# Half 0's scan groups 1 and 2 as one output product of eight k tiles, with the merge's first part stepped as its sums are finished

## The chip, the cores and the metric

The kernel runs on one core of one Trainium2 chip. The metric is the device time of one execution in microseconds (us); less is better.

## What is computed

One inference step of a small hybrid model: a SwiGLU block, then two branches (a pooling mixer and a Mamba-2 scan, "SSD") that sigmoid gates join, then a second SwiGLU block. All is float32. There are 1024 prompt tokens and 64 sample tokens (8 sequences of 8), `D_MODEL` is 1024. The change lies in the part behind the scan:

```python
yg = (y.reshape(Bsz, T, D_INNER) * jax.nn.silu(z))
yg = yg.reshape(Bsz, T, N_SSD_GROUPS, D_INNER // N_SSD_GROUPS)      # 4 groups of 512
yg = yg * lax.rsqrt(jnp.mean(yg * yg, axis=-1, keepdims=True) + EPS)
y = yg.reshape(Bsz, T, D_INNER) * ssd_norm
branch_ssd = y @ ssd_w_out                                          # 2048 x 1024
gates = jax.nn.sigmoid(gate_logits).reshape(Bsz, T, 2, D_MODEL)
merged = gates[:, :, 0] * branch_pool + gates[:, :, 1] * branch_ssd
return merged @ w_o, ...
```

## The kernel before

**Tiling.** Activations lie transposed, channels on the 128 partitions, tokens along the free dimension. The tokens are two halves: half 0 has 512 prompt tokens, half 1 the other 512 and the 64 sample tokens (576). A block of 128 channels is a k tile or, of an output, an m block. Each product of float32 numbers is made of three matmuls: every operand is split into a high and a low part (`split`, L370 on ScalarE for the high one, L374 on VectorE for the low one), and high x high, low x high and high x low are summed in PSUM (`products`). In half 0 an m block's sum takes one PSUM bank; four banks, of the kind `pd`, go round.

**The scan and its output product.** The scan goes through eight pieces in a fixed order, half 0's groups 0 to 3 and then half 1's. A group of the reference is four k tiles of `branch_ssd`'s product. The scan is a chain: a generator that is stepped in between the matmuls of the products (`tick`), each `yield x` saying after how many us of emitted matmuls the next step is due. So while TensorE makes half 0's output products, half 1's group 0 is scanned. In the profile the scan's names are `pxT`, `pcb`, `pst`, `pyo`, `pyd` (PSUM), `xdt`, `xd`, `ab`, `ea`, `cbm`, `hst` (VectorE and GpSimd). Behind the scan of each group comes `gating`: the gate (L1677), the sum of squares on VectorE (`ssq`, L395) and TensorE (`pss`), its root on GpSimd (`rsm`, L378), spread by TensorE (`prb`, L180), and the four splits (`yhl`, L374). The operands `yhl` lie in buffers of the kind `pair`, of which there are 8, one for a k tile's two parts: two groups at a time. The line `while h * NG + g - 2 >= freed[0]` holds the splits of a group back until the group two before it has been used by its output product; `freed` counts the groups used.

**SETS.** Of each half, `SETS` says which groups make an output product together. Half 0 has four sets of one group. The first three are made by `ssd_out`: for each of the eight m blocks a sum over four k tiles, which is put into `acc[m]` by ScalarE for group 0 (L1760) and added to `acc[m]` by VectorE for the others (L1762). `dense` loads the weights in two transfers for each m block and group. The last set is made by `merge`.

**The merge.** With t = 2 x sigmoid - 1 of the gate, kept in DRAM as `gd`, and the pooling branch's gated part as `accd`, it makes (t + 1) x (acc + pso) + ac. Its first part, `head`, is a chain of eight steps, one for each m block: load `t1` and `ac` (L1774, L1775; 256 KB each), then 2 us later on VectorE acc = (t1 + 1) x acc (L1777), and on GpSimd acc = acc + ac (L1778). It starts when the merge starts. The second part, for each m block: the sum `pso` over group 3's four k tiles, on VectorE t1 = (t1 + 1) x pso (L1791) and t1 = t1 + acc (L1792), and the split into `mh` and `ml` by 0.5, the operands of the next product (`pwo`, with `w_o`), whose sums use the same four `pd` banks.

**Order.** The order of each engine's instructions is set when the program is built: by the order in which the code and the chains emit them, and by a scheduler with priorities (`tc.high_priority`: evictions, HP_EV, go ahead). SyncE issues nearly all transfers in the order of its own queue.

## Time and profile before

| | |
|---|---|
| median of 3 runs | 2871.04 us (2869.55 to 2874.98) |
| the profiled execution's own time | 2877.41 us |
| its span in the trace | 2875.6 us |
| mean granted TensorE clock | 0.989 |
| output product of groups 1 and 2, half 0 | about 1714 to 1787 us of the span, for the part that follows group 1's first three blocks |
| merge of half 0 | 1787 to about 1850 us |

Engines are PE (TensorE's matmuls), PEld (its weight loads), DVE (VectorE), ACT (ScalarE), POOL (GpSimd) and SP (SyncE). PEclk is the TensorE clock that was granted, as a share of full speed. A group's row gives line, engine, operation, output and inputs, shapes and count, then the busy time in us, the mean in ns, and the idle time of the engine ahead of it with what ended most of that. A row of the timeline gives the start and the duration in us, and in brackets the idle time ahead of it and what ended it. A row of the waits gives who waited for whom: us in total, times, longest.

### The profile page before, as it was taken

What the parts mean: (1) busy time and instruction counts of PE and PEld (TensorE: products, weight loads), DVE (VectorE), ACT (ScalarE), POOL (GpSimd) and SP (SyncE); (2) the same over time, 40 slices, a digit from 0 to 9 for tenths busy, and PEclk for the clock granted to TensorE, in tenths of its full rate; (3) what the DMA queues carried; (4) which work ended last, traced back from release to release, by engine and by line L of the source; (5) the groups of instructions that cost most, each with busy time, mean ns of one, the idle gap of its engine ahead of it and who ended that gap; (6) DMA issues with size and microseconds to landing.
All of it is one profiled execution on the core that took longest, in us unless ns stands there. A gap on an engine that the chain in (4) does not pass through costs nothing.

```text
span 2875.6 us, 54690 instructions
## 1 busy us (share of the span) xinstructions
PE 2775.5 (97%) x19834; PEld 2606.6 (91%) x19834; DVE 1879.0 (65%) x2912; ACT 1364.5 (47%) x3024; POOL 1378.5 (48%) x1406
## 2 busy tenths in 40 slices
PE   7999999999999999999989999899999999999998
PEld 5999999899889999999988887678999999998997
DVE  6665565777884586867765767776665554457675
ACT  5444444643454565554554446556233434445433
POOL 6566566543442355554622332332235766664522
PEclk9999999999999999999999999999999999999999
DMA  4565554787745455544377788887775332337865
GB/s 132 180 209 193 175 161 151 248 295 250 238 130 161 154 167 168 180 155 137 100 234 231 213 251 268 261 272 216 235 242 176 107 99 94 99 114 257 286 202 183
DMA packets 533488, 548.02 MB, mean 191 GB/s; under 512 B 42836, under 2 KB 373704, under 8 KB 533208
## 3 DMA queue, kind: packets, MB, share of 16 engines
q1 hardware_dynamic: 533200, 544.51, 59.5%
q8 instruction: 156, 2.56, 0.4%
q14 instruction: 116, 0.95, 0.1%
q10 hardware_dynamic: 16, 0.00, 0.0%
HBM read 391.82 MB, written 152.78 MB: 189 GB/s over the span
## 4 chain that ended last, share of the span: by engine, by line
PE 75%; DMA 7%; DVE 6%; issue 4%; POOL 4%; ACT 2%; SPq 1%; POOLq 0%; ACTq 0%; DVEq 0%
PE pw L176 43%; PE po L176 10%; PE pso L176 5%; PE pg L176 3%; PE pbp L176 3%; PE pwo L176 3%; PE pu L176 2%; DMA hr<-xq 1%; PE pgm L176 1%; DMA hp<-xq 1%; PE pyd L176 1%; PE pst L176 1%; DVE hr L781 1%; DVE wl L459 1%; POOL s L676 1%
## 5 line engine op out<-in xcount | busy, mean ns | idle before, releaser
L176 PE MATMUL pw<-X,wh 128*128 128x288 f32 (+2 forms) x2832 | 627.5, 310 | 5.0 <-ACT t L604 2.7
L176 PEld LDWEIGHTS pw<-X,wh 128*128 128x128 f32 x2832 | 462.1, 189 | 27.3 <-ACT t L604 3.2
L176 PE MATMUL pw<-X,wl 128*128 128x288 f32 (+1 forms) x1644 | 473.6, 288 | 0.8 <-DVE wl L459 0.8
L459 DVE TENSOR_TENSOR wl<-s,wh 128x512 fp32r<-128x512 f32 x288 | 245.2, 853 | 247.1 <-ACT wh L458 232.4
L176 PE MATMUL pw<-hl,wh 128*128 128x256 f32 (+1 forms) x1536 | 391.7, 328 | 3.6 <-ACT t L580 2.3
L452 POOL TENSOR_TENSOR s<-wraw,wraw 128x512 f32<-128x512 f32 x144 | 198.9, 1381 | 332.8 <-DVE wl L459 210.3
L176 PE MATMUL pw<-hi,wh 128*128 128x288 f32 x1120 | 331.7, 296 | 2.6 <-DVE t L616 1.9
L176 PE MATMUL pw<-hi,wl 128*128 128x288 f32 x1120 | 329.8, 294 | 0.0
L176 PE MATMUL pw<-lo,wh 128*128 128x288 f32 x1120 | 329.6, 294 | 0.0
L176 PEld LDWEIGHTS pw<-X,wl 128*128 128x128 f32 x1644 | 311.7, 190 | 1.0 <-DVE wl L459 1.0
L176 PE MATMUL pw<-hl,wl 128*128 128x256 f32 x1072 | 300.6, 280 | 0.9 <-DVE wl L459 0.9
L176 PEld LDWEIGHTS pw<-hl,wh 128*128 128x128 f32 x1536 | 258.8, 189 | 24.9 <-ACT t L580 2.9
L759 POOL TENSOR_TENSOR ws<-wraw,wraw 128x512 f32<-128x512 f32 x120 | 179.8, 1507 | 200.9 <-DMA wraw<-in_ffn_w_out_dram 88.5
L459 DVE TENSOR_TENSOR wl<-wraw,wh 128x512 fp32r<-128x512 f32 x216 | 185.3, 858 | 124.2 <-ACT wh L458 118.9
L458 ACT ACTIVATE wh<-s 128x512 fp32r<-128x512 f32 x288 | 181.2, 630 | 136.2 <-PE pw L176 110.0
L176 PEld LDWEIGHTS pw<-hi,wh 128*128 128x128 f32 x1120 | 210.5, 188 | 9.5 <-DVE t L616 2.5
L176 PEld LDWEIGHTS pw<-lo,wh 128*128 128x128 f32 x1120 | 210.6, 188 | 0.0
L176 PEld LDWEIGHTS pw<-hi,wl 128*128 128x128 f32 x1120 | 210.1, 188 | 0.0
L458 ACT ACTIVATE wh<-wraw 128x512 fp32r<-128x512 f32 x216 | 135.8, 629 | 151.4 <-PE pw L176 130.7
L176 PEld LDWEIGHTS pw<-hl,wl 128*128 128x128 f32 x1072 | 202.9, 189 | 1.9 <-DVE wl L459 1.9
L176 PE MATMUL po<-hh,wh 128*128 128x272 f32 x848 | 179.9, 294 | 10.1 <-ACT wh L767 8.7
L176 PE MATMUL po<-hr,wh 128*128 128x272 f32 x848 | 178.1, 291 | 3.8 <-DVE hr L781 3.8
(403 smaller groups left out, 6773.3 us busy)
## 6 DMA issues: line engine op xcount, KB each, us to landing
wraw<-in_ffn_w_out_dram SPq DMA_DIRECT2D x240, 256.0 KB
wraw<-in_ffn_w_in_dram SPq DMA_DIRECT2D x188, 256.0 KB
wraw<-in_w_in_dram SPq DMA_DIRECT2D x144, 256.0 KB
wh<-part SPq DMA_DIRECT2D x116, 256.0 KB
wl<-part SPq DMA_DIRECT2D x116, 256.0 KB
hr<-xq SPq DMA_DIRECT2D x106, 272.0 KB
xq<-s SPq DMA_DIRECT2D x66, 272.0 KB
xq<-g SPq DMA_DIRECT2D x62, 272.0 KB
```

The lines of the kernel that those rows point to most:

```text
L176: T.matmul(out, lhsT, rhs, start=start, stop=stop, skip_group_check=free)
L452: G.tensor_tensor(t, a, b, op=op)
L458: S.activation(wh, a, AF.Copy)
L459: V.tensor_tensor(wl, a, wh.bitcast(F32), op=ALU.subtract)
L676: G.tensor_tensor(out[:, a], x0[:, a], y[:, b0], op=op)
L759: G.tensor_tensor(s, raws[0], raws[1], op=ALU.subtract if p in MINUS2 else ALU.add)
L781: V.tensor_tensor(t[:, :n].bitcast(F32R), t[:, :n], a[:, :n].bitcast(F32), op=ALU.subtract)
```

## The change

`SETS` of half 0 becomes (0), (1, 2), (3). `ssd_out` is written anew: for a set of several groups the first `N_LEAD` m blocks (three in half 0, one in half 1) are done group by group, with their banks kept open, so that the second group's operands are needed only behind three blocks of the first; the other blocks run over all k tiles at once. Each m block of groups 1 and 2 is then one sum of eight k tiles and one eviction into `acc[m]` where there were two: eight VectorE adds fewer in half 0. The number of matmuls and of weight loads stays. `freed` goes from 1 to 3 at once at the joint product's end.

`head` becomes `merge_head`. In half 0 it starts ahead of the joint product and not with the merge, and a step waits until its m block's sum has been evicted (`left`): the sixteen loads, the eight L1777 and the eight L1778 stand between the joint product's matmuls. In half 1 it starts where it did, ahead of the merge. From line 57 on, lines are one higher in the new kernel; L1777 and L1778 become L1763 and L1764, L1791 and L1792 become L1807 and L1808, the add of an eviction, L1762, becomes L1790.

```diff
-SETS = (((0,), (1,), (2,), (3,)), ((0, 1), (2,), (3,)))
+SETS = (((0,), (1, 2), (3,)), ((0, 1), (2,), (3,)))
+N_LEAD = (3, 1)
...
-    def ssd_out(h, gs, acc):
-
-        yn = ynorm(h, gs)
-        for m in range(KD):
-            pb = dense(ssd_w_out[0], gs[0] * 4, 4 * len(gs), m * P, [yn], name="pso")[0]
...
-        def head():
+    def merge_head(h, acc, left):
+
+        N, t1, count = NTOK[h], [None] * KD, [0]
+
+        def run():
             for m in range(KD):
                 t1[m], ac = act((P, N), name="t1"), act((P, N), name="ac")
                 dma(t1[m], gd[h][KD + m])
                 dma(ac, accd[h][m])
                 yield MP
+                while left[0] <= m:
+                    yield 1.0
                 V.scalar_tensor_tensor(acc[m], t1[m], 1.0, acc[m], op0=ALU.add, op1=ALU.mult)
                 G.tensor_tensor(acc[m], acc[m], ac, op=ALU.add)
-                merged[0] += 1
-
-        ch = start(head(), MP)
+                count[0] += 1
+
+        return start(run(), MP), t1, count
+
+    def ssd_out(h, gs, acc, left):
+
+        lead = N_LEAD[h] if len(gs) > 1 else 1
+        for ms in (tuple(range(lead)),) + tuple((m,) for m in range(lead, KD)):
+            pbs = [banks([(h,)], "pd", "pso")[0] for _ in ms]
+            for i, g in enumerate(gs):
+                _, yh, yl = scanned(h, g)
+                before_ = [None] * (4 * i)
+                for m, pb in zip(ms, pbs):
+                    wh, wl = load_w(ssd_w_out[0], g * 4, 4, m * P)
+                    for kk in range(4):
+                        products([pb], wh, wl, kk, slice(0, P), [(h, before_ + yh, before_ + yl)], 4 * i + kk, 4 * len(gs))
+                        tick()
...
+                left[0] += 1
+        freed[0] += len(gs)
+
+    def merge(h, gs, acc, first):
+
+        N = NTOK[h]
+        ch, t1, merged = first
...
         for gs in SETS[h][:-1]:
-            ssd_out(h, gs, acc)
-        mhl = merge(h, SETS[h][-1], acc)
+            left = [0]
+            if h == 0 and gs == SETS[h][-2]:
+                first = merge_head(h, acc, left)
+            ssd_out(h, gs, acc, left)
+        if h == 1:
+            first = merge_head(h, acc, left)
+        mhl = merge(h, SETS[h][-1], acc, first)
```

How the instructions move, at three places of VectorE's order. The first is the end of the product ahead of the merge. Before, from the last eviction (of `pso` into `acc_3881`, the eighth m block) on; all operands of the merge have been split by then:

```order
L1762 TENSOR_TENSOR acc_3875_21747<-acc_3875_21747,pso_22689 128x512
L1541 TENSOR_TENSOR ab_22629<-ab_22629,cbm_22663 128x512
L1541 TENSOR_TENSOR ab_22631<-ab_22631,cbm_22663 128x512
L1762 TENSOR_TENSOR acc_3881_21783<-acc_3881_21783,pso_22715 128x512
L395 TENSOR_TENSOR ssq_22733<-ssq_22733,sq_22735 128x576
L1638 TENSOR_TENSOR hst_22752<-hst_22752,pst_22750 128x512
L1520 TENSOR_TENSOR xdt_22767<-pxT_22755,dts_20160 128x512
L1513 TENSOR_TENSOR cbm_22763<-pcb_22760,tri 128x128
L1530 TENSOR_TENSOR xd_22769<-pxT_22755,dts_20160 128x512
L1541 TENSOR_TENSOR ab_22707<-ab_22707,cbm_22763 128x512
L1541 TENSOR_TENSOR ab_22709<-ab_22709,cbm_22763 128x512
```

After, the four splits of group 3 (`yhl` of 128x512) stand here:

```order
L375 SCALAR_TENSOR_TENSOR yhl_22753<-xs_3684_20737,cols,yhl_22753 128x512
L1542 TENSOR_TENSOR ab_22641<-ab_22641,cbm_22673 128x512
L375 SCALAR_TENSOR_TENSOR yhl_22757<-xs_3684_20737,cols,yhl_22757 128x512
L1542 TENSOR_TENSOR ab_22643<-ab_22643,cbm_22673 128x512
L1790 TENSOR_TENSOR acc_3881_21783<-acc_3881_21783,pso_22699 128x512
L396 TENSOR_TENSOR ssq_22747<-ssq_22747,sq_22749 128x576
L375 SCALAR_TENSOR_TENSOR yhl_22761<-xs_3684_20737,cols,yhl_22761 128x512
L375 SCALAR_TENSOR_TENSOR yhl_22765<-xs_3684_20737,cols,yhl_22765 128x512
L1521 TENSOR_TENSOR xdt_22799<-pxT_22787,dts_20160 128x512
L1514 TENSOR_TENSOR cbm_22795<-pcb_22792,tri 128x128
L1531 TENSOR_TENSOR xd_22801<-pxT_22787,dts_20160 128x512
L1807 SCALAR_TENSOR_TENSOR t_3899_21847<-t_3899_21847,pso_22769 128x512
```

Two of the splits come ahead of the last eviction and two behind it, and the first L1807 of the merge has moved ahead of the scan's `hst`.

The second place is the merge's start, from the last sum of squares of half 1's group 0 (`ssq`) to its mean (`rsm`), which the steps behind `prb` need. Before:

```order
L395 TENSOR_TENSOR ssq_22733<-ssq_22733,sq_22787 128x576
L1617 TENSOR_TENSOR ea_22633<-pyo_22823,ea_22633 128x512
L1777 SCALAR_TENSOR_TENSOR acc_3810_21468<-t_4100_22790,acc_3810_21468 128x512
L1618 TENSOR_TENSOR ea_22633<-ea_22633,pyd_22828 128x512
L1791 SCALAR_TENSOR_TENSOR t_4100_22790<-t_4100_22790,pso_22739 128x512
L1777 SCALAR_TENSOR_TENSOR acc_3822_21520<-t_4102_22802,acc_3822_21520 128x512
L1792 TENSOR_TENSOR t_4100_22790<-t_4100_22790,acc_3810_21468 128x512
L1513 TENSOR_TENSOR cbm_22883<-pcb_22880,tri 128x128
L1791 SCALAR_TENSOR_TENSOR t_4102_22802<-t_4102_22802,pso_22812 128x512
L374 SCALAR_TENSOR_TENSOR ml_22807<-t_4100_22790,mh_22806 128x512
L407 TENSOR_SCALAR rsm_22859<-pss_22853 128x4
L409 TENSOR_SCALAR rsm_22859<-pss_22853 64x1
```

After:

```order
L396 TENSOR_TENSOR ssq_22747<-ssq_22747,sq_22816 128x576
L1808 TENSOR_TENSOR t_3899_21847<-t_3899_21847,acc_3810_21468 128x512
L396 TENSOR_TENSOR ssq_22747<-ssq_22747,sq_22819 128x576
L1807 SCALAR_TENSOR_TENSOR t_3963_22145<-t_3963_22145,pso_22834 128x512
L375 SCALAR_TENSOR_TENSOR ml_22829<-t_3899_21847,mh_22828 128x512
L1618 TENSOR_TENSOR ea_22645<-pyo_22845,ea_22645 128x512
L408 TENSOR_SCALAR rsm_22875<-pss_22869 128x4
L1619 TENSOR_TENSOR ea_22645<-ea_22645,pyd_22850 128x512
L410 TENSOR_SCALAR rsm_22875<-pss_22869 64x1
```

Nine instructions stood between the last `ssq` and the first `rsm`, and three do now; an L1808 has come in ahead of that `ssq`.

The third place is the middle of the merge, from `hst` on, where the merge's `ml` and the evictions of `pso` stand among the scan's and the gating's instructions. Before:

```order
L1638 TENSOR_TENSOR hst_23010<-hst_23010,pst_23008 128x512
L1777 SCALAR_TENSOR_TENSOR acc_3863_21694<-t_4147_22983,acc_3863_21694 128x512
L374 SCALAR_TENSOR_TENSOR yhl_23058<-xs_3787_21312,cols,yhl_23058 128x576
L1792 TENSOR_TENSOR t_4126_22906<-t_4126_22906,acc_3846_21624 128x512
L1777 SCALAR_TENSOR_TENSOR acc_3875_21747<-t_4163_23044,acc_3875_21747 128x512
L1617 TENSOR_TENSOR ea_22844<-pyo_23085,ea_22844 128x512
L374 SCALAR_TENSOR_TENSOR ml_23066<-t_4126_22906,mh_23065 128x512
L1513 TENSOR_TENSOR cbm_23137<-pcb_23135,tri_s 64x64
L1618 TENSOR_TENSOR ea_22844<-ea_22844,pyd_23090 128x512
L1791 SCALAR_TENSOR_TENSOR t_4135_22941<-t_4135_22941,pso_23071 128x512
L1791 SCALAR_TENSOR_TENSOR t_4147_22983<-t_4147_22983,pso_23197 128x512
L1791 SCALAR_TENSOR_TENSOR t_4163_23044<-t_4163_23044,pso_23220 128x512
```

After:

```order
L375 SCALAR_TENSOR_TENSOR yhl_23050<-xs_3787_21312,cols,yhl_23050 128x576
L1808 TENSOR_TENSOR t_3977_22210<-t_3977_22210,acc_3846_21624 128x512
L1618 TENSOR_TENSOR ea_22866<-pyo_23071,ea_22866 128x512
L1807 SCALAR_TENSOR_TENSOR t_4009_22326<-t_4009_22326,pso_23063 128x512
L1514 TENSOR_TENSOR cbm_23121<-pcb_23119,tri_s 64x64
L375 SCALAR_TENSOR_TENSOR ml_23058<-t_3977_22210,mh_23057 128x512
L1619 TENSOR_TENSOR ea_22866<-ea_22866,pyd_23076 128x512
L1807 SCALAR_TENSOR_TENSOR t_4018_22383<-t_4018_22383,pso_23181 128x512
L1807 SCALAR_TENSOR_TENSOR t_4053_22559<-t_4053_22559,pso_23204 128x512
```

The two L1777 here (of `acc_3863` and `acc_3875`, the sixth and seventh m block) are gone; in the new order they stand ahead of the merge, as do the other six but the last, which stands just behind its first product.

More of the change, by code (lines that the diff above doesn't have):

```diff
@@ L1748, in ynorm @@
         return h, sum((y[1] for y in ys), []), sum((y[2] for y in ys), [])
-    def ssd_out(h, gs, acc):
-        yn = ynorm(h, gs)
-        for m in range(KD):
-            pb = dense(ssd_w_out[0], gs[0] * 4, 4 * len(gs), m * P, [yn], name="pso")[0]
-            if gs[0] == 0:
-                acc[m] = act((P, NTOK[h]), name="acc2")
-            with tc.high_priority(HP_EV):
-                for pt, (a, b) in zip(pb, PIECES[h]):
-                    if gs[0] == 0:
-                        S.copy(acc[m][:, a:b], pt[:, : b - a])
-                    else:
-                        V.tensor_tensor(acc[m][:, a:b], acc[m][:, a:b], pt[:, : b - a], op=ALU.add)
-        freed[0] += len(gs)
-    def merge(h, gs, acc):
-        N = NTOK[h]
-        t1 = [None] * KD
-        merged = [0]
-        def head():
+    def merge_head(h, acc, left):
+        N, t1, count = NTOK[h], [None] * KD, [0]
+        def run():
             for m in range(KD):
@@ L1776, in head @@
                 yield MP
+                while left[0] <= m:
+                    yield 1.0
                 V.scalar_tensor_tensor(acc[m], t1[m], 1.0, acc[m], op0=ALU.add, op1=ALU.mult)
                 G.tensor_tensor(acc[m], acc[m], ac, op=ALU.add)
-                merged[0] += 1
-        ch = start(head(), MP)
+                count[0] += 1
[12 more added lines that the diff above has]
+                        tick()
+            for m, pb in zip(ms, pbs):
+                if gs[0] == 0:
+                    acc[m] = act((P, NTOK[h]), name="acc2")
+                with tc.high_priority(HP_EV):
+                    for pt, (a, b) in zip(pb, PIECES[h]):
+                        if gs[0] == 0:
+                            S.copy(acc[m][:, a:b], pt[:, : b - a])
+                        else:
+                            V.tensor_tensor(acc[m][:, a:b], acc[m][:, a:b], pt[:, : b - a], op=ALU.add)
+                left[0] += 1
[3 more added lines that the diff above has]
+        ch, t1, merged = first
         yn = ynorm(h, gs)
```

## The prediction

> **What bounds the kernel now.** I read the page first, for what is busy over the whole span.
>
> ```profile
> span 2875.6 us, 54690 instructions
> PE 2775.5 (97%) x19834; PEld 2606.6 (91%) x19834; DVE 1879.0 (65%) x2912; ACT 1364.5 (47%) x3024; POOL 1378.5 (48%) x1406
> ```
>
> TensorE is busy in 97% of the span, and the change leaves its matmuls as they are. Time can come only from stretches in which TensorE waits, or runs at a lower granted clock. So the next view is the sums by windows for the three stretches that the change touches: the second and third groups' product of half 0 (1714 to 1787), the merge of half 0 (1787 to about 1850), and what follows it.
>
> ```profile
> core 0: us, PE busy (x) PEld busy (x) DVE busy (x) ACT busy (x) POOL busy (x), PEclk, DMA share, GB/s
> 1714.00:1787.00 73.00, 71.42 (x481) 56.80 (x480) 57.09 (x90) 44.09 (x122) 27.12 (x24) 1.00 0.87 262
> 1787.00:1850.00 63.00, 55.08 (x297) 41.90 (x296) 55.69 (x82) 29.73 (x77) 29.25 (x21) 0.92 0.84 278
> 1850.00:1910.00 60.00, 55.46 (x378) 41.88 (x378) 41.53 (x65) 37.40 (x101) 20.74 (x16) 1.00 0.85 263
> ```
>
> In the first stretch TensorE is idle for 73.00 - 71.42 = 1.6 us only. In the merge it is idle for 63.00 - 55.08 = 7.9 us, its clock is granted at 0.92 (worth up to 63 x 0.08 = 5.0 us), and VectorE has 55.69 us of work in 63. So at most 7.9 + 5.0 = 12.9 us can be had in the merge. The waits of TensorE in these two stretches, the merge's first, say who ends the idle time:
>
> ```profile
> PE prb L180 <- POOL rsm L378: 2.2, 1, 2.2
> PE pst L176 <- DVE xd L1530: 2.1, 1, 2.1
> PE pwo L176 <- DVE t L1791: 2.1, 1, 2.1
> PE pcb L176 <- DVE ea L1617: 0.7, 1, 0.7
> PE pwo L176 <- DVE ml L374: 0.6, 1, 0.6
> ```
>
> ```profile
> PE prb L180 <- POOL rsm L378: 0.8, 1, 0.8
> PE ph0T L180 <- DMA h<-in_state_ssm_dram: 0.8, 1, 0.8
> ```
>
> Four of the merge's five waits are for VectorE, 5.5 us together; the fifth is for a small GpSimd step. In the earlier stretch neither wait is for an eviction.
>
> **The evictions.** Eight adds of a 128x512 sum into `acc` go. The groups by line in the earlier stretch:
>
> ```profile
> L1762 DVE TENSOR_TENSOR acc<-acc,pso 128x512 f32<-128x512 f32 x15 | 10.2, 680 | 2.5 <-PE pso L176 2.5
> L374 DVE SCALAR_TENSOR_TENSOR yhl<-xs,cols,yhl 128x512 fp32r<-128x512 f32 x4 | 3.0, 746 | 0.4 <-ACT yhl L370 0.4
> ```
>
> They free 8 x 0.68 = 5.4 us of VectorE. VectorE is idle there for 73.00 - 57.09 = 15.9 us and no wait of TensorE is for it, so I count them at nothing. If that cover were gone they would be worth the 5.4.
>
> **The merge's first part.** In the merge it is these rows, of VectorE and of GpSimd:
>
> ```profile
> L1777 DVE SCALAR_TENSOR_TENSOR acc<-t,acc 128x512 f32<-128x512 f32 x8 | 6.5, 808 | 0.0
> L1778 POOL TENSOR_TENSOR acc<-acc,ac 128x512 f32<-128x512 f32 x8 | 13.6, 1707 | 17.3 <-DVE acc L1777 17.3
> ```
>
> 6.5 us of VectorE and 13.6 of GpSimd leave the merge for the joint product, with 16 loads of 256 KB. Not all of the 6.5 pays: an instruction counts only where VectorE runs without a gap and TensorE waits at its end. That is the stretch from 1816.13 to 1835.94, here by its first row, some inside, and its last, the third of three together:
>
> ```profile
> 1816.13 0.29 DVE L1513 TENSOR_TENSOR cbm<-pcb,tri 128x128 f32<-128x128 f32 x1 [3.12 <-PE pcb L180]
> 1820.11 1.85 DVE L1686 TENSOR_TENSOR xs<-xs,r 128x576 f32<-128x576 f32 x1
> 1825.33 0.75 DVE L1686 TENSOR_TENSOR xs<-xs,r 128x576 f32<-128x576 f32 x1
> 1827.93 0.68 DVE L1530 TENSOR_TENSOR xd<-pxT,dts 128x512 f32<-128x512 f32 x1
> 1832.26 1.17 DVE L374 SCALAR_TENSOR_TENSOR ml<-t,mh 128x512 fp32r<-128x512 f32 x1
> 1834.08 1.86 DVE L1791 SCALAR_TENSOR_TENSOR t<-t,pso 128x512 f32<-128x512 f32 x3
> ```
>
> Three of TensorE's waits end on its rows:
>
> ```profile
> 1828.75 2.05 PE L176 MATMUL pst<-xd,btok 128*128 128x512 f32 x2 [2.09 <-DVE xd L1530]
> 1832.39 0.33 PE L176 MATMUL pcb<-bc,bc 128*64 128x64 f32 x2 [0.74 <-DVE ea L1617]
> 1834.80 0.50 PE L176 MATMUL pwo<-mh,wh 128*128 128x512 f32 x1 [2.08 <-DVE t L1791]
> ```
>
> By the order, 27 instructions stand behind that `cbm` up to the third L1791; after the change 23 do. Three L1777 are gone, and one add to `ea` stands ahead of the `cbm`, where VectorE sits idle for 3.12 us. At the 0.6 us from one to the next (three in 1.86), that is 4 x 0.6 = 2.4 us. More goes with the GpSimd adds. Two of them run here:
>
> ```profile
> 1819.66 1.68 POOL L1778 TENSOR_TENSOR acc<-acc,ac 128x512 f32<-128x512 f32 x1 [1.30 <-DVE acc L1777]
> 1829.88 4.66 POOL L1778 TENSOR_TENSOR acc<-acc,ac 128x512 f32<-128x512 f32 x2 [7.02 <-DVE acc L1777]
> ```
>
> The L1686 that begins beside the first takes 1.85 us against 0.75 without one (1.1 more), and `ml` beside the second 1.17 against the 0.68 of its neighbours (0.5 more). The Trainium skill, page "SBUF — State Buffer", section "SBUF: two separate sides", says that a VectorE instruction with two inputs in SBUF and a GpSimd instruction that reads SBUF hold one pair of ports in turn, the loser fully blocked. The trace agrees by its sign, with 1.1 us; by that rule the price isn't removed but goes with the adds into the earlier stretch, which is the slower rival below.
>
> So VectorE is done here 2.4 + 1.6 = 4.0 us earlier. Of TensorE's 2.09 + 0.74 + 2.08 = 4.9 us, 4.0 go; about 0.9 at the first `pwo` stays. Behind it, one L1777 less in VectorE's queue takes 0.6 us, the `ml` wait.
>
> **From the merge's start to `prb`.** Here the change adds. The last of group 3's four splits before, and the merge's first product with its third k tile:
>
> ```profile
> 1762.52 0.75 DVE L374 SCALAR_TENSOR_TENSOR yhl<-xs,cols,yhl 128x512 fp32r<-128x512 f32 x1 [0.40 <-ACT yhl L370]
> 1787.10 0.61 PE L176 MATMUL pso<-yhl,wh 128*128 128x512 f32 x2
> 1790.00 0.70 PE L176 MATMUL pso<-yhl,wh 128*128 128x512 f32 x2
> ```
>
> The splits were done 24 us ahead of that product; now they stand right ahead of the merge's first product, since its buffers come free only as the joint product's last sum reads group 1 for the last time. Four splits of 0.75 are 3.0 us, two of them behind the last eviction, which waits for that sum. TensorE needs the third of them only 2.9 us into the merge (two k tiles and the scan's steps lie between), when the last eviction, an `ssq` add and that split (0.7 + 0.75 + 0.75) are just done, so it waits 0 to 1 us for them. But the `ssq` sums are queued behind them on VectorE, and `pss` waits for those:
>
> ```profile
> 1793.31 1.61 DVE L395 TENSOR_TENSOR ssq<-ssq,sq 128x576 f32<-128x576 f32 x2
> 1795.07 1.23 PE L176 MATMUL pss<-ones,ssq 128*128 128x1 f32 x10
> 1799.13 1.74 POOL L1778 TENSOR_TENSOR acc<-acc,ac 128x512 f32<-128x512 f32 x1
> 1802.29 1.62 POOL L378 TENSOR_TENSOR rsm<-rsm,mhalf 128x5 f32<-128x5 f32 x1
> 1803.96 0.32 PE L180 MATMUL prb<-ident,rsm 128*128 128x128 f32 x1 [2.15 <-POOL rsm L378]
> ```
>
> By the order VectorE has two splits, an L1791, an L1777 and an L1792 more between the last eviction and the last `ssq`: 2 x 0.75 + 3 x 0.6 = 3.3 us. `ssq` ended at 1794.92, just ahead of `pss`, so `pss` waits up to 3 us where it waited for nothing. What is lost there is mostly given back at `prb`: behind the last `ssq`, nine instructions stood ahead of `rsm` on VectorE and three do now (two L1777, an L1791, an L1792 and two steps of the scan are elsewhere), and the add of 1.74 us isn't ahead of it on GpSimd. So `pss` waits 2 to 3, `prb` 0.5 to 1 instead of 2.15: net **+1 us**, between -1.5 (no new wait) and +3 (nothing given back).
>
> **The clock.** Two windows of 5 us in the merge, and one in the stretch before:
>
> ```profile
> 1805.00:1810.00 5.00, 5.00 (x16) 3.93 (x16) 3.93 (x7) 2.36 (x7) 2.39 (x3) 0.68 0.96 327
> 1835.00:1840.00 5.00, 5.00 (x20) 4.00 (x20) 4.68 (x7) 1.34 (x5) 4.10 (x4) 0.66 0.99 279
> 1770.00:1775.00 5.00, 4.21 (x31) 2.91 (x32) 1.80 (x3) 5.00 (x16) 0.00 (x0) 1.00 1.07 337
> ```
>
> Behind the 2.15 us wait at 1803.96 and behind the three that end at 1834.80 TensorE is busy throughout at 0.68 and 0.66, so each costs 5 x 0.33 = 1.6 us. Behind idle time of 0.8 us, at 1770, the clock stays at 1.00. If the second group of waits shrinks from 4.9 to 0.9 its dip goes: **-1.6 us**. The first I leave, as `pss` and `prb` still wait some 3 us. The Trainium skill, page "TensorE: Matmul & The Clock Gate", section "What's actually happening", has the clock fall after at least one idle window of some 3.4 us in a free-running frame; the longest single wait here is 2.15 us, so by it neither dip should be there, this term would be 0, and the sum 1.6 us less. The rows show both, and I go by them.
>
> **The joint product.** It takes the eight steps on VectorE and GpSimd and 16 loads into a stretch whose transfers have a share of 0.87 and a clock at 1.00. VectorE's sum there moves little (-5.4 for evictions, +6.5 for eight steps). What can be late are the state load at 0.8 us (its issue is queued behind more loads on SP) and GpSimd's steps on the carried state. No row before shows it; the nearest are the two 0.8 us waits. From 0 to three such more, 2.4; I take **+0.5**. Group 2's use costs nothing: it is read first after three blocks of group 1, at the place in TensorE's order where group 1's fourth block stood, so later than before.
>
> **Sum.** -4.0 - 0.6 + 1.0 - 1.6 + 0.5 = -4.7, say -5, and the order behind the merge is the same, so that it carries through to the end. The profiled execution took 2877.41 us, 6.4 more than the median of the runs, 2871.04; against the median -5 gives **2866 us**. About 0.2% (5.7 us) is what a measurement here can tell from no change, so the forecast lies just inside.
>
> **Rivals.**
> - *The clock and `prb` come back in full.* If TensorE's wait at `pss` doesn't appear (VectorE has idle time that takes the splits), `prb` falls to the 0.8 us of the earlier stretch and both dips go: -4.9 - 0.6 - 1.4 - 3.2 - 1 for the later stretch = -11, 2860 us. For it: the earlier stretch holds the same scan steps at 1.00. Against: 3.3 us more are queued ahead of `ssq`. Chance 0.15.
> - *The relief is eaten by the next wait.* TensorE gets to `pwo` 3 us earlier and waits there for `ml` or for the state chain of half 1; the dip stays. Then -4.0 - 0.6 + 2 + 1.6 = -1, 2870 us. For it: three waits in a row that all end on one engine. Chance 0.12.
> - *Slower: GpSimd's adds hold up half 1's scan.* The eight adds, 13.6 us, stand in the joint product ahead of GpSimd's steps on the carried state and the gate, which TensorE needs within each scan unit; each add also blocks one VectorE step by 1.1 us. If 11 us of these 13.6 + 8.8 lie on the path, that outweighs the -4.7 and gives +6, 2877 us; it decides from 0.6 us of new wait per add. Against it: in the merge GpSimd's adds held TensorE once in eight times, at `prb`. Chance 0.13.
> - That the change doesn't do what it says is excluded by the order, which has eight evictions fewer and the steps moved.
>
> **Numbers.** The likeliest case has 0.60; its own range is +1 to -9 by the bounds above (-4.6 + 3 + 2.4, and -4.6 - 1.5 - 3.2), somewhat less than half of it beyond 5.7. Faster: 0.28 + 0.15 = 0.43. Same: 0.32 + 0.12 = 0.44. Slower: 0.13. The range goes from some 14 us below the median, past the first rival, to 3 above, which leaves out most of the slower one: 2857 to 2874.
>
> **What would show it.** Right: no `pst<-xd` wait near 2 us and no dip behind the merge's second half; `prb` under 1.2; a new `pss<-ssq` wait of 2 to 3; 1714 to 1787 no more than 1 us longer. Wrong: `pwo` waiting 3 us or more, or TensorE's idle time in the joint product over 4 us.

## The result, and the profile after

The changed kernel takes 2866.77 us (median of 20 runs, 2860.67 to 2876.58) against 2871.27 (20 runs, 2865.16 to 2876.78): a ratio of 0.9982, 95% interval 0.9975 to 0.9989, or 4.5 us less by the medians and 5.2 by the ratio. Two more comparisons with further runs gave 0.9990 (0.9981 to 0.9999) and 0.9993 (0.9984 to 1.0002), that is 2.9 and 2.0 us less, the last with 1 inside its interval. The prediction was 2866, 5 us less. Its number came out, much of its working did not.

The profiled execution took 2863.49 us. The page's first lines, after:

```profile
span 2861.7 us, 54691 instructions
PE 2766.0 (97%) x19834; PEld 2595.6 (91%) x19834; DVE 1867.4 (65%) x2904; ACT 1362.0 (48%) x3024; POOL 1367.7 (48%) x1406
```

The eight adds are gone (2912 to 2904 instructions on VectorE). The sums by windows, in the same three stretches as before the change:

```profile
1714.00:1787.00 73.00, 69.25 (x468) 54.25 (x466) 57.63 (x84) 40.17 (x114) 34.19 (x29) 1.00 0.91 283
1787.00:1850.00 63.00, 56.23 (x313) 42.03 (x313) 54.47 (x85) 34.33 (x89) 16.96 (x15) 0.97 0.81 251
1850.00:1910.00 60.00, 56.78 (x397) 43.02 (x395) 42.92 (x68) 34.66 (x94) 22.01 (x17) 0.97 0.86 267
```

In the joint product TensorE is idle for 3.75 us (1.6 before), in the merge for 6.8 (7.9 before), and the merge's clock is 0.97 where it was 0.92. GpSimd's work in the merge fell from 29.25 to 16.96 us, VectorE's hardly (55.69 to 54.47): the stretch now gets further into the work behind it. The waits of TensorE after, in the joint product and in the merge:

```profile
PE pb L181 <- DVE hst L1639: 0.8, 1, 0.8
PE px L181 <- DVE xdt L1521: 0.7, 1, 0.7
PE pst L177 <- DVE xd L1531: 0.7, 1, 0.7
PE prb L181 <- POOL rsm L379: 0.6, 1, 0.6
PE px L181 <- DVE ea L1619: 0.6, 1, 0.6
PE pb L181 <- DVE cbm L1514: 0.4, 1, 0.4
```

```profile
PE pss L181 <- POOL rsm L379: 2.3, 1, 2.3
PE pso L177 <- DVE yhl L375: 1.7, 2, 1.2
PE pso L177 <- DMA wl<-part: 1.0, 1, 1.0
PE pst L177 <- DVE xd L1531: 0.7, 1, 0.7
...
```

The waits of 2.1 us at `pst` and `pwo` are a third of what they were or gone. In their place stand five new ones for VectorE's scan steps in the joint product (3.2 us together), two at the merge's first product for the late splits, one for weights, and the one for `rsm` is as long as before.

**Where the time went.** A trace's stretches can be compared to a few tenths of a microsecond, where the clock falls at the same places, if they are cut at the scan's steps, which every variant has, and not at times. I take the time since the `pst` at 1710.55 us (of before; 1707.34 after), add or subtract 0.227 us for each 512-column product matmul that the variant has done fewer or more by then (three of them take 0.68 us from one k tile's row to the next), and subtract the same of the first trace of before. Positive is late. Three traces of each kernel, by the time of before at which the step stands:

```
step, at us of before      before 1   2      3     after 1   2      3
state step ph0T    1764.2    0.00   0.28  -0.15     3.79   3.84   3.82
last group's pcb   1780.6    0.00   0.21   0.46     2.31   2.36   2.34
pst in the merge   1788.5    0.00   0.21   0.45     4.04   4.08   4.05
prb                1804.0    0.00   0.21   0.45     8.21   8.18   8.43
pst behind prb     1813.6    0.00   0.15  -1.17     6.15   6.11   6.35
ph0T, merge's end  1844.2    0.00   0.30  -0.88    -0.75  -0.77  -0.55
pcb                1871.7    0.00   0.03  -1.11    -1.05  -0.66  -0.97
pcb                1938.2    0.00  -0.67  -1.13    -0.85  -1.58  -2.36
pcb                1966.3    0.00  -0.88  -1.22    -3.98  -3.78  -5.19
```

The change loses 2.3 us in the joint product, 1.7 at the merge's first product, 4.1 more up to `prb`, and wins 9.0 from there to the merge's end. Some 2 us of the 4.1 and of the 9.0 are a dip of the clock (a stretch at half speed) that has changed its place. Before, it lies just behind `prb` (1805 to 1810 at 0.68, and in the third trace not at all); after, it lies just ahead of it, in all three traces:

```profile
1800.00:1805.00 5.00, 5.00 (x20) 3.53 (x20) 2.86 (x7) 0.00 (x0) 0.00 (x0) 0.66 1.10 306
```

At the `pst` behind `prb` both have had theirs: by that cut the change loses 2.1 us from the merge's first product on and wins 6.9 from there. At the merge's end half a microsecond is left (0.75, 1.07 and -0.33 by pairs). A further 3 us are won behind the merge, up to 1966, and 2.0 in the second SwiGLU block: from the last `pwo` to that block's first `po` the three traces before take 477.7, 477.8 and 477.7 us, the three after 475.4, 475.7 and 476.0.

### The profile page after: what moved, and what is told of

It reads as the page before. It is cut to its first block, busy times and chain, and to the rows that moved or that the text cites. A ratio compares the mean times of both kernels' runs of the same rounds, so it can differ in the third digit from the quotient of the medians.

```text
span 2861.7 us, 54691 instructions
## 1 busy us (share of the span) xinstructions
PE 2766.0 (97%) x19834; PEld 2595.6 (91%) x19834; DVE 1867.4 (65%) x2904; ACT 1362.0 (48%) x3024; POOL 1367.7 (48%) x1406
## 4 chain that ended last, share of the span: by engine, by line
PE 74%; DMA 9%; DVE 6%; issue 4%; POOL 3%; ACT 3%; SPq 1%; POOLq 0%; ACTq 0%; DVEq 0%
PE pw L177 45%; PE po L177 8%; PE pso L177 4%; PE pg L177 3%; PE pbp L177 3%; PE pwo L177 3%; PE pu L177 2%; DMA hr<-xq 2%; DMA hp<-xq 1%; DMA ea<-eacd 1%; DMA wraw<-in_ffn_w_out_dram 1%; PE pgm L177 1%; DMA ab<-acsd 1%; DVE hr L782 1%; PE pyd L177 1%
## 5 line engine op out<-in xcount | busy, mean ns | idle before, releaser
L760 POOL TENSOR_TENSOR ws<-wraw,wraw 128x512 f32<-128x512 f32 x120 | 172.0, 1440 | 204.4 <-DVE wl L769 74.7
L460 DVE TENSOR_TENSOR wl<-wraw,wh 128x512 fp32r<-128x512 f32 x216 | 178.3, 825 | 125.3 <-ACT wh L459 120.5
L177 PE MATMUL pso<-yhl,wh 128*128 128x288 f32 (+1 forms) x768 | 179.2, 338 | 2.1 <-DVE yhl L375 1.7
```

The source lines that it names most:

```text
L177: T.matmul(out, lhsT, rhs, start=start, stop=stop, skip_group_check=free)
L460: V.tensor_tensor(wl, a, wh.bitcast(F32), op=ALU.subtract)
L760: G.tensor_tensor(s, raws[0], raws[1], op=ALU.subtract if p in MINUS2 else ALU.add)
```

## The experiments

One table for all, read like the one above:

```
                            1764   1780   1788   1804   1844   1966   ratio of the times (95%)
changed kernel              3.79   2.31   4.04   8.21  -0.75  -3.98   0.9982 (0.9975 to 0.9989)
joint product alone        -0.16  -1.47  -1.46  -1.65   1.46  -2.50   0.9998 (0.9989 to 1.0007)
first part alone            1.33   2.08   5.00   8.95   0.50  -2.26   1.0003 (0.9992 to 1.0013)
changed, GpSimd adds late   3.83   2.39   4.09   8.33   0.53  -4.38   0.9983 (0.9974 to 0.9992)
joint, loads twice          2.26   0.80   1.35   0.95   7.60   2.39   one run, 2874.97 us
changed, first four early   3.82   2.39   2.40   6.58  -0.33  -0.31   0.9994 (0.9985 to 1.0003)
changed, rsm ahead          3.81   2.35   4.28   7.64  -0.69  -5.53   0.9984 (0.9975 to 0.9993)
the same, GpSimd adds late  3.83   2.36   4.07   6.23  -1.95  -3.25   0.9990 (0.9981 to 0.9999)
before, rsm ahead          -0.14  -0.14  -0.14  -0.65  -0.27  -5.49   1.0006 (0.9997 to 1.0015)
```

The two rows with late adds are not variants of their own: every engine has its instructions in the order of the changed kernel in the first, and in that of the run with `rsm` ahead in the second. They are further traces and times of these two.

**The changed kernel again** (`c1_after_again`), for the noise of a trace.

> The changed kernel once more, for a second trace. I cut the trace at two scan steps of half 1's group 0 that every variant has: the `pst` two k tiles into the merge (1788.46 us before, 1789.30 after) and the first state transpose `ph0T` of the sample part of half 1 (1844.17, 1837.72), counted from the `pst` at 1710.55 (1707.34) and up to the last `pcb` at 1966.26 (1958.45). Joint product and merge's start: 77.9 before, 82.0 after. Merge: 55.7, 48.4. What follows: 122.1, 120.7. Sum 255.7, 251.1. Every theory expects these three to come again within 1 us each, and a ratio of 0.998. If they differ by 2 us or more between two traces of one kernel, no cause can be read from a single trace of a variant.

Up to the merge's end the two traces agree within 0.2 us, and within 1.4 behind it. The ratio was 0.9990. So what a variant does up to the merge's end can mostly be read from one trace; what it does behind it, less surely. The two runs with late adds, which repeat programs already traced, set the bound: where the clock falls once more or for longer, two traces of one program differ by 1.3 to 1.4 us at `prb` or at the merge's end.

**One part alone: the joint product** (`e1_joint_head_late`).

```diff
-            if h == 0 and gs == SETS[h][-2]:
-                first = merge_head(h, acc, left)
             ssd_out(h, gs, acc, left)
-        if h == 1:
-            first = merge_head(h, acc, left)
+        first = merge_head(h, acc, left)
```

> One part alone: groups 1 and 2 as one product of eight k tiles, but the merge's first part starts with the merge, as before. My theory (the gain is VectorE's and GpSimd's work taken out of the merge): the joint product is shorter than in the changed kernel by 1 to 2 us, the late splits stay; the merge is as long as before, 55 to 58 us, with waits of 2 us at `pst` and `pwo` again; total 0 to 3 us above the kernel before, ratio 1.000 to 1.001. The rival (the eight saved evictions on VectorE are the gain): total 3 us or more below the kernel before, ratio 0.999 or less.

2868.52 us, a ratio of 0.9998, good to 2.6 us. Eight evictions fewer, with the late splits in them, are worth nothing that the times can tell; the rival, which needed 3 us, falls. The joint product by itself is 1.5 us ahead at the merge's start, late splits and all, and the merge then loses it. Its waits in the merge, and the clock there:

```profile
PE pst L177 <- DVE xd L1531: 4.2, 1, 4.2
PE pcb L177 <- DVE ea L1618: 4.1, 1, 4.1
...
```

```profile
1825.00:1830.00 5.00, 1.78 (x6) 0.58 (x4) 5.00 (x5) 2.46 (x6) 4.99 (x3) 0.50 0.29 71
1830.00:1835.00 5.00, 4.00 (x13) 3.07 (x14) 4.00 (x8) 1.23 (x5) 3.42 (x3) 0.50 0.49 151
```

VectorE is busy for 9.0 of these 10 us, GpSimd for 8.4, its adds among that, and TensorE, which got there sooner, waits twice as long for the same `xd`. That is the backlog that the prediction spoke of, and no `rsm` wait is left ahead of it.

**The other part alone: the first part early, one group at a time** (`e2_head_early_single`).

```diff
-SETS = (((0,), (1, 2), (3,)), ((0, 1), (2,), (3,)))
+SETS = (((0,), (1,), (2,), (3,)), ((0, 1), (2,), (3,)))
```

> The other part alone: four sets of one group as before, and the merge's first part started ahead of group 2's product and stepped as its sums are added. The splits of group 3 stand where they stood before. My theory: the merge is as short as in the changed kernel, 48 to 50 us, its start doesn't wait for splits (1.7 us less than in the changed kernel), so 4 to 7 us below the kernel before, ratio 0.9975 to 0.9986, equal to the changed kernel or a little better. The rival (evictions): within 1 us of the kernel before, ratio 0.9995 to 1.0005.

2869.76 us, 1.0003: my expectation was wrong. From `prb` to the merge's end it wins 8.5 us, as I thought, but it is 5.0 us behind at the merge's `pst` and 9.0 at `prb`, though its splits stand early. Its waits from the merge's start on:

```profile
PE pst L177 <- ACT ab L1540: 2.8, 1, 2.8
PE pso L177 <- DMA wh<-part: 2.4, 1, 2.4
...
```

A loss at the merge's start thus comes without late splits, and the joint product alone has late splits without a loss. In the changed kernel 1.2 of the 1.7 us there still end on the late `yhl`, with the moved steps ahead of them on VectorE. With single groups the sums are finished later, and VectorE's first step of the moved part comes 36 instructions later than in the changed kernel; the steps begin at 1757 us of its trace and not at 1735, three of the eight fall into the merge's start, and VectorE itself waits for their loads:

```profile
1757.03 0.68 DVE L1763 SCALAR_TENSOR_TENSOR acc<-t,acc 128x512 f32<-128x512 f32 x1
...
1791.91 1.77 DVE L1763 SCALAR_TENSOR_TENSOR acc<-t,acc 128x512 f32<-128x512 f32 x1 [0.72 <-DMA t<-gd]
```

**GpSimd's adds back in the merge** (`e4_gpsimd_add_late`): meant to leave VectorE's steps early, with the adds emitted by a second chain that starts with the merge.

```diff
                 V.scalar_tensor_tensor(acc[m], t1[m], 1.0, acc[m], op0=ALU.add, op1=ALU.mult)
-                G.tensor_tensor(acc[m], acc[m], ac, op=ALU.add)
-                count[0] += 1
+                done[0] += 1
...
+        def adds():
+            for m in range(KD):
+                yield MP
+                while done[0] <= m:
+                    r.step()
+                G.tensor_tensor(acc[m], acc[m], acs[m], op=ALU.add)
+                count[0] += 1
...
```

> The changed kernel with one half of the moved steps put back: VectorE's product (t + 1) x acc stays early, GpSimd's adds of `ac` stand in the merge again, 2 us apart from its start. VectorE's order is the one of the changed kernel. By my sum, VectorE's instructions were worth 2.4 us of the merge's stretch and GpSimd's contention 1.6, and the joint product gets shorter by what the adds cost it there. So the merge is 2 to 3 us longer than in the changed kernel (50 to 52), the joint product 1 to 2 shorter: total within 2 us of the changed kernel. A rival that holds GpSimd alone for the cause: the merge is 55 or more again and the total that of the kernel before. A rival that holds the order on VectorE alone for it: the merge is unchanged at 48 to 49 and the total 1 to 2 us under the changed kernel.

This run doesn't test what it was meant to. The adds are emitted later, but the order that was built is that of the changed kernel on every engine, and in the trace the adds run where they ran (the whole trace is 1.4 us earlier). First the changed kernel, then this run:

```profile
L1764 POOL TENSOR_TENSOR acc<-acc,ac x8: 1264/1279/1739, 1736.3 to 1795.3; 128x512 f32<-128x512 f32 x8
```

```profile
L1775 POOL TENSOR_TENSOR acc<-acc,ac x8: 1266/1280/1738, 1734.9 to 1793.9; 128x512 f32<-128x512 f32 x8
```

So it is the changed kernel once more, with a ratio of 0.9983 and alike up to `prb` to 0.1 us. That it stands 1.3 us later at the merge's end (0.53 against -0.75) is no price of the adds: behind `prb` its clock falls a second time,

```profile
1805.00:1810.00 5.00, 2.81 (x9) 2.32 (x10) 2.85 (x5) 4.74 (x14) 3.24 (x4) 0.71 1.11 307
```

where the changed kernel has 1.00, and from the `pst` behind `prb` on both win 6.9 us. What the adds cost, in the joint product or in the merge, no run here shows.

**The loads** (`e11_joint_loads_twice`): the joint product with the first part in the merge, and the sixteen loads issued early as well, into buffers that nothing reads.

```diff
+    def idle_loads(h, left):
+        for m in range(KD):
+            t, ac = act((P, NTOK[h]), name="t1"), act((P, NTOK[h]), name="ac")
+            dma(t, gd[h][KD + m])
+            dma(ac, accd[h][m])
+            yield MP
+            while left[0] <= m:
+                yield 1.0
...
```

> Where the loss at the merge's start comes from. This is the joint product with the merge's first part left in the merge, and in addition the sixteen loads of 256 KB at the places of the changed kernel, into buffers that nothing reads (the merge loads them again). Without these loads the variant was 1.5 us ahead of the kernel before at the `pst` in the merge's start and 1.7 ahead at `prb`; the changed kernel was 4.0 and 8.2 behind. If the transfers are the cause (share over 1.0, weights late by 1 to 2.7 us), this run is 3 to 8 us behind at `prb`. If VectorE's moved instructions are, it is within 1 us of the variant without the loads, some 1.5 ahead of before.

Neither end: against the joint product alone the loads cost 2.4 us by 1764, 2.8 at the merge's `pst` and 2.6 at `prb`. Against the same, the changed kernel is 5.5 and 9.9 behind. So the early loads are about half of what is lost up to the merge's start and a quarter at `prb`; they act early, in the joint product. By 1829 this run is worse by 9.6 us than without them, with a wait of 6.0 us for `xd`. It carries 4 MB more than any other, and its extra tiles take buffers of the kind that the scan and the merge use; I have no cause for that, and the run doesn't part the transfers from the buffers.

**Half of the moved part** (`e13_first4_early`): the loads and steps of m = 4 to 7 wait for the merge.

```diff
             for m in range(KD):
+                while h == 0 and m >= 4 and not begun[0]:
+                    yield 1.0
                 t1[m], ac = act((P, N), name="t1"), act((P, N), name="ac")
...
```

> Half of the moved part: the first four m blocks' loads and steps in the joint product, the other four with the merge as before. My theory, now with the loss at the merge's start seen: the steps of the last m blocks, which come when VectorE has the late splits, delay `ssq` and `rsm`; without them the merge's start loses 4 us less than in the changed kernel, while the second half of the merge keeps half or more of the gain (four L1763 fewer in it). So the total is 1 to 3 us below the changed kernel, ratio to the kernel before 0.997 to 0.9982. A rival in which the loss at the start is due to the earlier second part of the merge (L1807, L1808 no longer held up): the loss stays at 8 us at `prb`, and the total is 0 to 3 us above the changed kernel.

0.9994, no better than before. At the merge's `pst` it is 1.6 us better than the changed kernel, where 4 were expected at the merge's start, and that is all: up to `prb` it loses 4.2 more, as the changed kernel does, and the rival is nearer there. The wait for `rsm` is the longest of all runs:

```profile
PE pss L181 <- POOL rsm L379: 3.7, 1, 3.7
PE pst L177 <- DVE xd L1531: 1.7, 1, 1.7
```

What the runs that lose time up to `prb` have in common is that the merge's second part can start at once: L1807 and L1808 of the first m blocks stand ahead of the last `ssq` and of `rsm`. In the joint product alone they come behind. No run moves them by themselves, so that they are the cause is argued and not shown.

**`rsm` at a higher priority** (`e14_rsm_up`, `e15_rsm_up_add_late`, `e16_before_rsm_up`), in the changed kernel, in that with the late adds, and in the kernel before. In the changed kernel GpSimd did this, ready for `rsm` at 1802.3:

```profile
1802.12 0.14 DVE L410 TENSOR_SCALAR rsm<-pss 64x1 f32<-64x1 f32 x1
1805.43 1.04 POOL L1533 TENSOR_TENSOR xs<-xs,Dcol 128x512 f32<-128x512 f32 x1 [8.84 <-PE pxT L181]
1806.43 1.27 POOL L1620 TENSOR_TENSOR xs<-xs,ea 128x512 f32<-128x512 f32 x1
1807.65 1.18 POOL L379 TENSOR_TENSOR rsm<-rsm,mhalf 128x5 f32<-128x5 f32 x1
1808.89 0.27 PE L181 MATMUL pss<-ident,rsm 64*128 64x64 f32 x1 [2.28 <-POOL rsm L379]
```

(the last row is TensorE's, from the timeline of the same trace.) On GpSimd `rsm` stands in the order behind a step that waits for TensorE's `pxT`, and it started at 1807.65, 5.4 us after it was ready.

```diff
-        V.tensor_scalar(sm[:, 2, :4], pt[:, :4], 1.0 / count, EPS, op0=ALU.mult, op1=ALU.add)
...
-        rsqrt(sm[:, 0, :nch], v)
+        with tc.high_priority(up):
+            V.tensor_scalar(sm[:, 2, :4], pt[:, :4], 1.0 / count, EPS, op0=ALU.mult, op1=ALU.add)
...
+            rsqrt(sm[:, 0, :nch], v)
...
```

> The changed kernel, and the three small steps behind `pss` of half 1's first group (the mean on VectorE, the root `rsm` on GpSimd) at a higher priority: `rsm` moves on GpSimd from behind a step that waits for `pxT` (L1533) and a gate step (L1620) to ahead of both. If the wait of 2.28 us at `prb` in the changed kernel comes from GpSimd's order, it goes below 0.5, the ledger at `prb` is 1.5 to 2.5 us better than the changed kernel's +8.2 and stays so to the merge's end: total 1 to 3 us below the changed kernel, ratio to the kernel before 0.997 to 0.998. If TensorE waits for something else there as long (hst, weights), the total is that of the changed kernel.

> The same, and GpSimd's adds of `ac` in the merge again. With the adds late the changed kernel was level with itself (0.9983 beside 0.9990 of the unaltered one in the same call, both against the kernel before), 1.3 us worse at the merge's end. I expect the two edits to add: at the merge's end 0 to 1 us worse than the run with the priority alone, total within 1.5 us of it.

> The kernel before, with `rsm` at the higher priority: on GpSimd it moves ahead of two adds of `ac` (L1778) and two scan steps. Its wait at `prb` was 2.15 us, followed by a dip of the clock of 1.6. If the prediction had the place right (an add of 1.74 us ahead of `rsm`), the wait falls to 0.8 or less and `prb` comes 1.4 to 2 us sooner; whether the dip goes too shows what a wait of that length costs with and without. Total 1 to 3 us below the kernel before if VectorE's backlog behind it doesn't take it back, 0 if it does (VectorE's waits at `pst` and `pwo` then grow by as much).

In the changed kernel the wait went, as expected, but `prb` gained 0.6 us and not 2:

```profile
...
PE pss L181 <- POOL rsm L379: 0.4, 1, 0.4
```

Counted from the same `pst`, VectorE's mean was done 0.7 us sooner and `rsm` began 6.0 sooner. What took most of the gain is the clock's dip at this place, which lasts longer here, worth 3.3 us by these windows where the changed kernel's is worth 1.7:

```profile
1805.00:1810.00 5.00, 4.65 (x13) 2.92 (x12) 2.07 (x4) 0.69 (x2) 1.31 (x1) 0.50 1.09 310
1810.00:1815.00 5.00, 5.00 (x38) 4.32 (x38) 3.81 (x7) 2.79 (x9) 3.38 (x4) 0.84 1.10 321
```

The run with the adds late too has this run's order on every engine, so it is a second trace of it. There the dip is the shorter one (0.66 in one window), `prb` gains the 2 us (6.23 against 8.2 to 8.4), and at the merge's end it stands at -1.95 (-0.69 in the first trace), where 0 to 1 us worse than the first was expected. The ratios, 0.9984 and 0.9990, are not to be told from the changed kernel's. In the kernel before, `prb` came only 0.5 us sooner, and the next step 2.5, as the dip behind `prb` went too (1805 to 1810 at 1.00 and not 0.68). The gain was handed back to VectorE's backlog, now in one piece:

```profile
PE pcb L176 <- DVE ea L1618: 5.5, 1, 5.5
PE pst L176 <- DVE xd L1531: 1.4, 1, 1.4
...
```

At the merge's end it stands at -0.27, and the time is 1.0006. This is the clearest sign that in the kernel before VectorE sets the pace from the merge's start on: taking a wait from TensorE ahead of that lengthens the next one. In the changed kernel TensorE waits only 0.9 us between `prb` and the merge's end, and what `rsm` won at `prb` in its second trace is in good part still there at that end (-1.95).

**Second and third traces** (`c0_before_again`, `c2_after_third`, `c2_before_third`), on whether the gain behind the merge is the change's.

> The kernel before once more, for a second trace of it. At equal product work, the changed kernel and both of its parts are 2.3 to 3 us ahead between 1938 and 1966 us, far behind the change, where the trace of before shows clock dips of 0.68 and 0.84 and the trace after shows none. If those dips belong to one execution, this trace shows other ones and the gain there goes; if they belong to the kernel, it shows the same within 0.5 us. The merge itself (1788 to 1844) should come again within 1 us in both cases.

> A third trace of the changed kernel and more times. At the merge's end the two traces of it were 0.75 and 0.77 us ahead of the first trace of before at equal work, and 1.05 and 1.07 ahead of the second; between there and 1966 us they gained 3 more, and 2.1 to 2.2 in the second SwiGLU block, where a wait for ScalarE is 1.4 to 1.7 us without a clock dip, against 2.3 with one. If these are the change's, the third trace shows all three again: 0.7 to 1.1, 2 to 3.5, and 2; if the later two are the luck of single executions, at least one of them is gone. Ratio of the times 0.9975 to 0.9989 in the first and again here.

> A third trace of the kernel before, for the same. If the later gains are the change's, the wait for ScalarE in the second SwiGLU block is 2.2 to 2.4 us with a dip behind it, and the stretch from 1872 to 1966 is within 1 us of the first two traces.

A gain is there in all three pairs, but the third trace after is not what was expected: 0.55 us ahead of the first trace of before at the merge's end (0.7 to 1.1 expected), 4.6 more up to 1966 (2 to 3.5), 1.7 in the second SwiGLU block (2), with a ratio of 0.9993 (0.9975 to 0.9989). Between 1938 and 1966 the traces before lose or win at most 0.2 us against each other and those after are 2.2 to 3.1 better; over the whole stretch from 1872 the traces before stay within 0.9. The waits of TensorE there, of before and of the third trace after:

```profile
PE pst L176 <- ACT ab L1540: 1.8, 1, 1.8
PE pss L176 <- DVE ssq L395: 1.3, 1, 1.3
PE pso L176 <- ACT acc L1760: 0.5, 1, 0.5
```

```profile
PE pst L177 <- DVE xd L1531: 1.9, 1, 1.9
PE prb L181 <- DVE hst L1639: 0.8, 1, 0.8
```

All three traces before wait for ScalarE's eviction and for `ssq`, and each has two or three windows of 5 us with a clock of 0.50 to 0.84 there; those after have one (0.69) or none. But the joint product alone and the first part alone show much of it too (they go from 1.46 and 0.50 at the merge's end to -2.50 and -2.26), and the kernel before with `rsm` ahead shows 5 us of it, while the times of these three are those of the kernel before. The two traces of the changed kernel with `rsm` ahead, one program, win 4.8 and 1.3 us there. The second SwiGLU block is no better tied to the change: the two runs with one part alone and that with half of the moved part take 475.4 to 475.6 us, at times that are not below those of before, and the two with `rsm` ahead, which hold the whole change, take 477.6. So neither gain is shown to be the change's, one trace of a variant is not enough behind the merge, and why the two parts together are faster by 2 to 5 us when neither is by itself stays open.

## Why the prediction was right, point by point

- **The number.** 5 us less were forecast, 4.5 came (0.9982, and 0.9983, 0.9990 and 0.9993 in the repeats), inside the range and the way it was forecast. That it came so close is luck, as the last but one point shows.
- **The evictions at nothing.** Held, as far as the times can tell: the joint product alone is at 0.9998. It won 1.5 us ahead of the merge, which the merge's backlog took.
- **The merge from `prb` on: -4.0, -0.6, and -1.6 for the clock.** The direction and the place were right: from the `pst` behind `prb` to the merge's end TensorE waits 0.9 us instead of 4.9, `pst` 0.7 instead of 2.1, and the dips of 0.66 to 0.87 in the second half are gone, in three traces. After:

```profile
1825.00:1830.00 5.00, 5.00 (x25) 3.67 (x24) 4.72 (x9) 1.79 (x5) 0.00 (x0) 1.00 0.39 125
1830.00:1835.00 5.00, 4.83 (x31) 3.75 (x29) 4.19 (x8) 1.59 (x6) 2.87 (x3) 1.00 0.93 285
...
```

  The size was near: 6.9 us from the `pst` behind `prb` on, for 6.2. The 9.0 from `prb` itself has the moved dip in it. The step from VectorE to TensorE was only half right. From the `cbm` to the last of the three evictions that the prediction counted (L1791, now L1807) VectorE took 19.8 us in all three traces before and takes 16.4 in all after: 3.4 of the 4.0.

```profile
1815.20 0.29 DVE L1514 TENSOR_TENSOR cbm<-pcb,tri 128x128 f32<-128x128 f32 x1 [0.37 <-PE pcb L181]
1830.32 1.27 DVE L1807 SCALAR_TENSOR_TENSOR t<-t,pso 128x512 f32<-128x512 f32 x2
```

  But it began 2.3 us later, counted from the same `pst`, and so was done only 1.2 sooner (1.3 against the second trace of before, and level with the third). Much of what TensorE won was thus its own lateness, which its waits for VectorE took up. The other runs bear that out: at the `pst` behind `prb` they stand from 3.7 us ahead to 7.4 late, and at the merge's end all but the one with the loads twice are within 2 us of the kernel before. The clock's -1.6 counted one dip. The rows of before from 1825 to 1840 (0.87, 0.79, 0.66) are two, worth up to 3.4 us; its second trace has one. GpSimd's part, put at 1.6, is shown by no run.
- **From the merge's start to `prb`: net +1.** Wrong, and the step that failed most: 1.7 us at the first product and 4.1 behind it, or 2.1 without the dip that moved. I had charged the late splits and let `rsm` pay back. The joint product alone has the splits as late and loses nothing. In the changed kernel TensorE waits 1.7 us for the splits, 1.0 for weights and 2.3 for `rsm`; the merge's own second part, free to start at once, stands ahead of `ssq` and `rsm`, which is argued to be part of it. And `rsm` paid nothing back, as on GpSimd it moved behind a step that waits for TensorE. That `prb` would wait 0.5 to 1 us was wrong (2.3), and so was the `pss` wait of 2 to 3: TensorE's order put a product there instead.
- **The joint product: +0.5.** It was 2.3, near the upper end given (2.4) and over the 1 us that was named as a sign. Against the joint product alone it is 3.8, of which the loads are 2.3, by the run with loads only. The rest is of another kind than foreseen: the three leading sums end together, and three L1763 stand among the scan's steps within 5 us:

```profile
1744.19 0.68 DVE L1763 SCALAR_TENSOR_TENSOR acc<-t,acc 128x512 f32<-128x512 f32 x1
1745.39 1.37 DVE L1763 SCALAR_TENSOR_TENSOR acc<-t,acc 128x512 f32<-128x512 f32 x1
1748.72 1.63 DVE L1763 SCALAR_TENSOR_TENSOR acc<-t,acc 128x512 f32<-128x512 f32 x1
```

  Two of them take 1.4 and 1.6 us beside a GpSimd add, for 0.7 of the first. Whether that is on the path, no run shows.
- **"Carries through to the end."** Wrong in both directions. The -4.7 that the sum has at the merge's end is -0.5 there, and about 3 us behind the merge and 2 in the second SwiGLU block came on top, for which the prediction had nothing and which no run ties to the change. The total was right because costs that were too low by 4.6 us (1.5 for 6.1), a gain that was too low by 0.7 and later gains that were not foreseen nearly cancel: luck.
- **Slower by GpSimd's adds.** It didn't come, as the total is shorter. How much the adds cost is not shown.

## What to carry to other kernels

Work moved out of a crowded stretch is paid for where it lands: read the engine's queue there too, instruction by instruction, and charge its loads. Where an engine paces a stretch, a wait removed ahead of it only lengthens the next one, so count the gain at the stretch's end and not wait by wait. To find where a small gain lies, cut several traces of each kernel at steps that both have, at equal work: total times differ by up to 16 us from run to run here, while these cuts repeat to 0.3 us as long as the clock falls at the same places, and to about 1.5 us where it doesn't, over 130 us. Before you read an experiment, see in its trace that the instructions stand where the edit was to put them: two of the runs here changed the order of no engine.

## What the runs showed of the hardware

The clock's dip is not a matter of the wait's length alone. The prediction took a dip for certain behind a wait of 2 us. In the changed kernel TensorE waited 2.28 us up to 1808.89, and the window around it has

```profile
1805.00:1810.00 5.00, 2.72 (x17) 2.06 (x16) 1.61 (x4) 3.50 (x11) 4.41 (x4) 1.00 1.07 344
```

and none of the five behind it is lower. The dip at this place came earlier, at 1800 to 1805 (0.66), where the longest wait of TensorE in the 5 us ahead was 1.05 us:

```profile
1799.81 0.50 PE L177 MATMUL pso<-yhl,wl 128*128 128x512 f32 x1 [1.05 <-DMA wl<-part]
```

The other two traces after have it at the same step, behind waits of 0.97 and 1.25 us. A place in the second SwiGLU block shows best how the length counts, as every variant waits there for the same step of ScalarE. Two traces of before, with the third one's window behind the wait, and one after:

```profile
2218.15 0.80 PE L176 MATMUL pw<-X,wh 128*128 128x512 f32 x1 [2.28 <-ACT v L576]
```

```profile
2213.93 0.50 PE L176 MATMUL pw<-X,wh 128*128 128x512 f32 x1 [2.27 <-ACT v L576]
...
2215.00:2220.00 5.00, 5.00 (x25) 4.63 (x25) 4.24 (x5) 1.63 (x4) 5.00 (x6) 0.70 0.34 116
```

```profile
2209.27 0.50 PE L177 MATMUL pw<-X,wh 128*128 128x512 f32 x1 [1.39 <-ACT v L577]
...
2210.00:2215.00 5.00, 5.00 (x36) 4.72 (x35) 5.00 (x6) 1.97 (x5) 5.00 (x6) 1.00 0.37 126
```

Over fourteen traces, the five with a wait of 1.39 to 1.70 us have no dip; of the nine with 1.89 to 2.35 seven have one and two (2.00 and 2.28) don't. A dip cuts the matmuls of a 5 us window from 36 to 25. That place alone is the 2.0 us in the second block. The Trainium skill, page "TensorE: Matmul & The Clock Gate", section "What's actually happening", has the activity counted in windows of some 3.4 us that run freely, so that, by it, where a wait falls in the window matters as well as its length. The traces agree that length alone doesn't decide between 1.9 and 2.3 us, nor for the dips behind 1 us; that a window must be idle as a whole, as the page's table reads, they don't bear out, with dips behind waits of 1 to 2 us.
